# Sparse attention layer of a decoder trunk: compressed tokens and gate columns as weights with hi and lo halves side by side, compressed keys appended to the first keys

## The chip, the cores and the metric

The kernel runs on one core of a Trainium2 chip. The metric is the device time of one execution in microseconds (us); the time of a kernel is the median of its runs. The engines are named TensorE (PE; its weight loads PEld), VectorE (DVE), ScalarE (ACT), GpSimd (POOL) and SyncE (SP, which issues the weight transfers).

## What is computed

Four decoder layers over 256 tokens of width 2048: stick-breaking attention, native sparse attention, gated spatial mixing, stick-breaking attention again. Each layer adds its mixer's output and a gated projection of a per-layer input to `x`. The change is in the second layer, the sparse attention (16 heads in 4 groups of 4 that share keys and values), of which this matters:

```python
# compressed keys and values: 15 blocks of 32 tokens, stride 16
def compress_blocks(kv, blk_idx, pos, w1, w2):
    blocks = kv[:, blk_idx] + pos[:, None, :]
    flat = blocks.transpose(0, 1, 3, 2, 4).reshape(B, n_cmp, G, CMP_LEN * Dh)
    return gelu(flat @ w1) @ w2
gates = sigmoid(g).reshape(B, S, 3, G, HG)
s_c = einsum('bqgnd,bcgd->bgnqc', qf, kc) - slopes * dist_c      # 15 compressed keys
p_c = softmax(where(mask_c, s_c, NEG)) * mask_c
s_s = einsum('bqgnd,bgqtd->bgnqt', qf, k_g) - slopes * dist_s    # selected keys
s_w = einsum('bqgnd,bkgd->bgnqk', qf, k_b) - slopes * dist_w     # window keys
o = gate_c * (p_c @ vc) + gate_s * (p_s @ v_s) + gate_w * (p_w @ v_w)
y = (o * silu(z)) @ w_out
```

All is float32 in the reference. The kernel keeps that precision on TensorE by splitting an operand into a rounded part (hi, type fp32r) and the rest (lo), and adding the products hi*hi, hi*lo and lo*hi.

## The kernel before, in words

**Units.** The whole program is a list of units. A unit is 1024 columns of a weight array: SyncE loads two units with one transfer (`load`), `cut` splits a unit into `wh` (ScalarE copy, L80) and `wl` (VectorE subtraction, L81), and a function issues its matmuls. `run` walks the units in order. At unit `i` it first issues the cuts up to unit `i + 3` (`SPLIT_AHEAD = 3`, four buffers, so that cut `i + 3` waits until TensorE is done with unit `i - 1`), then calls `resume`, then issues the unit's own matmuls. `resume` takes one step in each open generator, the oldest first. A `yield` in a generator so ends its part of one unit. All engines execute in the order in which this walk issues. One such stop, from one unit to the next, is called a step below.

**Tiles.** `fm` computes 128 output features for 256 tokens with two units, each of 8 pairs of matmuls of 512 and 256 columns (L212, L214), and hands the sum in PSUM to a generator: `joined` adds its two halves (ScalarE L248, VectorE L249), `scaled` multiplies by the norm (L255). `tm` computes values, token-major, with 8 units of 12 matmuls (L236 to L238).

**The sparse layer** (`nsa`). First come 8 units of values, the four tiles of keys to be compressed (`cmp_tiles(0)`), 8 units of values, the four compression units of the keys (`cmp_units(0)`), the four tiles and later the four units of the values to be compressed, and between them the gate columns (`gate_unit`, 16 pairs on 48 output rows). `cmp_post` adds the positions to the last tile's windows (VectorE, 8 instructions, L692) and `cmp_unit` multiplies with float32 weights that are not cut: 8 matmuls of 60 columns for each unit, which appear as 16 instructions (L707).

**The heads.** Then 16 heads follow. Each has the two units of its query tile and two units of a fill tile (a gate tile `z` for heads 3, 4, 6, 7, 8, 10 to 15, else a key tile). Its generator `q_post` and `attend` take one step for each of these parts:

- 0: query scaled; 1: query split; 2: nothing
- 3: scores on TensorE into PSUM banks A and B: three 512-column and three 256-column matmuls, and two float32 ones of 15 columns against `kc` (L837)
- 4: VectorE adds slopes and takes the maxima (L853, L855); 5: six exponentials on ScalarE (L863)
- 6: VectorE scales the probabilities (L866 to L875); 7: nothing
- 8: TensorE transposes them into banks C and D (L887, L888); 9: nothing
- 10: banks C and D are copied out in turns, ScalarE `ptc`, VectorE `ptc`, ScalarE `pt`, VectorE `pt`, ScalarE `pt1`, first C, then D (L89, L91, L80, L81, L897); 11: nothing
- 12: product with the values (TensorE, bank E, L903 to L907); 13: output copied (L911)

A head takes four steps, so that its neighbour is always four steps behind it: with steps named after the head's own number modulo four, step 0 holds one head's query, the next older head's maxima and the transposes of the one before, and so on. `z_post` multiplies the output by the gate on GpSimd once it is there, and splits it.

Of the kernel before, what the change touches and what calls it, by code (L numbers as in the profile page):

```python
# [16 lines left out]
P = 128  # L17
# [8 lines left out]
NCMP = 15  # L26
CMP_LEN = 32
# [13 lines left out]
class Trunk:  # L41
# [576 lines left out]
    def nsa(self, layer, act_in, act_out):  # L618
# [10 lines left out]
        def begin():  # L629
# [4 lines left out]
            st["kc"] = m.tile([P, G, NCMP], F32, name="kc")  # L634
# [24 lines left out]
            st["raw"] = [c.tile([P, G, S], F32, name=f"raw{b}") for b in range(2)]  # L659
            st["pos"] = [c.tile([P, CMP_LEN], F32, name=f"pos{b}") for b in range(2)]  # L660
            st["w2"] = [c.tile([P, HD], F32, name=f"w2{b}") for b in range(2)]
            st["h3"] = c.tile([P, G, 4, 32], F32, name="h3")
# [15 lines left out]
        def cmp_post(b, g):  # L678
            def gen(ps):
                t = st["raw"][b]  # L680
                self.scaled(ps, self.rb, t[:, g])
                if g == G - 1:

                    x = st["c"].tile([P, CMP_LEN, G, NCMP], F32, name="win")
                    st["win", b] = x
                    half = CMP_STRIDE
                    for i in range(CMP_LEN // half):
                        src = t[:, :, i * half:i * half + NCMP * half].rearrange(
                            "p g (c l) -> p l g c", l=half)
                        ps_ = st["pos"][b][:, i * half:(i + 1) * half]  # L690
                        for g2 in range(G):
                            nc.vector.tensor_add(  # L692
                                x[:, i * half:(i + 1) * half, g2], src[:, :, g2],
                                ps_[:, :, None].to_broadcast([P, half, NCMP]))
                return
                yield
            return gen

        def cmp_unit(b, q):
            def pe(raw, _):  # L700
                if q == 0:
                    st["cps", b] = self.bank("AB"[b])
                ps = st["cps", b]
                n = G * NCMP
                for j in range(8):
                    l = 8 * q + j
                    mm(ps[:, :n], raw[:, j * P:(j + 1) * P],  # L707
                       st["win", b][:, l].rearrange("p g c -> p (g c)"), start=l == 0,
                       stop=l == CMP_LEN - 1)
                if q == 3:  # L710
                    self.bg.append(cmp_gen(b, ps))
            return pe

        def cmp_gen(b, ps):
            n = G * NCMP
            if b == 0:
                h = st["c"].tile([P, n], F32, name="cmp_h")
                nc.scalar.activation(h, ps[:, :n], AF.Gelu)
            else:
                h3 = st["h3"]  # L720
                h = ps[:, :n].rearrange("p (g c) -> p g c", g=G)
# [36 lines left out]
        def gate_unit(wh, wl):  # L758
            n = 3 * H
            ps = self.acc.tile([P, 2, S], F32, name="acc")  # L760
            for k in range(KT):
                c = slice(k * n, (k + 1) * n)
                mm(ps[:n], wh[:, c], act_in[:, k], start=k == 0, stop=False,
                   skip_group_check=True)
                mm(ps[:n, 0], wl[:, c], act_in[:, k, 0], start=False, stop=k == KT - 1,
                   skip_group_check=True)
            self.bg.append(gate_post(ps))

        def gate_post(ps):
            n = 3 * H  # L770
            t = st["c"].tile([n, S], F32, name="g_lo")
            e = st["c"].tile([n, S], F32, name="g")
            nc.scalar.activation(t, ps[:n, 1], AF.Copy)
            nc.vector.tensor_add(e, ps[:n, 0], t)
            nc.vector.tensor_mul(e, e, self.rb[:n])
            nc.scalar.activation(e, e, AF.Exp, scale=-1.0)
            nc.vector.tensor_scalar(e, e, 1.0, None, op0=ALU.add)
# [47 lines left out]
        def attend(h, q, qs):  # L825
# [5 lines left out]
            kh, kl = keys(g)  # L831
            self.mm3(sa.rearrange("p (b s) -> p b s", b=2), (qs[:, 0, P:], qs[:, 1, P:]), (kh, kl),
                     start=True, stop=True)
            self.mm3(sb[:, :S].rearrange("p (b s) -> p b s", b=2), (qs[:, 0, :P], qs[:, 1, :P]),
                     (kh[:, :, :P], kl[:, :, :P]), start=True)
            for i in range(2):
                mm(sb[:, S + i * NCMP:S + (i + 1) * NCMP], q[:, i * P:(i + 1) * P], st["kc"][:, g],  # L837
                   start=False, stop=i == 1, skip_group_check=True)
# [11 lines left out]
                     sb[:, S:S + 2 * NCMP].rearrange("p (b s) -> p b s", b=2), mx[:, :, 0]))  # L850
# [81 lines left out]
        self.unit(a["nsa_g"], KT * 3 * H, gate_unit)  # L932
# [205 lines left out]
```

## Time and profile before

| | us |
|---|---|
| median of 3 runs | 2246.32 (2246.31 to 2246.91) |
| the profiled execution's own time | 2246.55 |
| its span in the profile | 2244.8 |
| TensorE busy | 2220.6 (99%) |
| VectorE busy | 1490.7 (66%) |
| ScalarE busy | 1227.8 (55%) |
| TensorE's granted clock over the span | 0.998 of full speed |

The profile is of one execution. Busy time is the time in which an engine has an instruction in work; matmuls are pipelined, so that the distance from one start to the next, not the duration, tells what one costs. A wait is idle time and what ended it. The chain of waits follows the work that ended last back to its start.

### The profile page before, as it was taken

Reading aid. Unit: us, or ns where it says so; the run is one execution under the profiler, and the core shown is the slowest. Engines: PE = TensorE matmul, PEld = TensorE weight load, DVE = VectorE, ACT = ScalarE, POOL = GpSimd, SP = SyncE. Lnnn points to the kernel's source line nnn. Section 1 sums busy time; section 2 is a strip of 40 time slices with the busy share of each in tenths; the row PEclk is TensorE's granted clock in tenths of the full one; section 3 lists DMA queues with packets and bytes.
Section 4 is the critical chain, followed back from the end, with each engine's and each line's share of the span. In section 5 each row is a group of like instructions: output and inputs, shape, how many; then the busy total and the mean of one; then the engine's idle time right before and its main releaser. Section 6 shows DMA issues by size and latency. Waiting matters only on the chain.

```text
span 2244.8 us, 32505 instructions
## 1 busy us (share of the span) xinstructions
PE 2220.6 (99%) x12664; PEld 1940.8 (86%) x12664; DVE 1490.7 (66%) x2242; ACT 1227.8 (55%) x2031; POOL 187.1 (8%) x203
## 2 busy tenths in 40 slices
PE   8999999999999999999999999999999999999997
PEld 6888888888888888888888888888888888888886
DVE  7655656657656788886675566666766566567666
ACT  6555556546544566654555555544555555555464
POOL 2000000002200011230121000000310000000022
PEclk9999999999999999999999999999999999999999
DMA  7455454555555434345556555555554544445552
GB/s 255 164 187 169 170 175 163 188 188 187 195 188 197 149 140 151 132 169 188 187 186 222 193 174 188 172 188 186 189 191 169 188 165 173 171 167 188 188 188 104
DMA packets 106522, 400.13 MB, mean 178 GB/s; under 512 B 7936, under 2 KB 8448, under 8 KB 106112
## 3 DMA queue, kind: packets, MB, share of 16 engines
q1 hardware_dynamic: 105792, 397.34, 51.2%
q8 instruction: 100, 1.64, 0.3%
q10 hardware_dynamic: 576, 0.70, 0.1%
q14 instruction: 54, 0.44, 0.1%
HBM read 395.92 MB, written 2.10 MB: 177 GB/s over the span
## 4 chain that ended last, share of the span: by engine, by line
PE 91%; DVE 4%; ACT 3%; issue 1%; DMA 0%; DVEq 0%; SPq 0%; ACTq 0%
PE acc L212 47%; PE acc L214 24%; PE acc L236 4%; PE acc L237 4%; PE acc L238 4%; DVE wl L81 1%; ACT wh L80 1%; ACT p L863 1%; PE ps_A L96 1%; PE ps_A L97 1%; PE ps_A L98 0%; PE ps_B L96 0%; PE ps_B L98 0%; PE ps_B L97 0%; DVE p L875 0%
## 5 line engine op out<-in xcount | busy, mean ns | idle before, releaser
L212 PE MATMUL acc<-act,wh 128*128 128x512 f32 x4864 | 1719.4, 395 | 0.0
L214 PE MATMUL acc<-act,wl 128*128 128x256 f32 x4864 | 1374.6, 283 | 0.0
L81 DVE TENSOR_TENSOR wl<-raw,wh 128x1024 fp32r<-128x1024 f32 (+1 forms) x738 | 927.7, 1261 | 596.8 <-ACT wh L80 596.5
L80 ACT ACTIVATE wh<-raw 128x1024 fp32r<-128x1024 f32 (+1 forms) x738 | 776.5, 1056 | 790.1 <-PE acc L212 459.2
L212 PEld LDWEIGHTS acc<-act,wh 128*128 128x128 f32 x4864 | 913.7, 188 | 206.2
L214 PEld LDWEIGHTS acc<-act,wl 128*128 128x128 f32 x4864 | 914.7, 188 | 0.4
L236 PE MATMUL acc<-wh,act 128*128 128x512 f32 x448 | 178.5, 398 | 5.9 <-ACT wh L80 5.9
L237 PE MATMUL acc<-wl,act 128*128 128x512 f32 x448 | 178.1, 397 | 2.1 <-DVE wl L81 2.1
L238 PE MATMUL acc<-wh,act 128*128 128x512 f32 x448 | 177.2, 396 | 0.0
L321 POOL TENSOR_TENSOR ssq<-x 128x256 f32<-128x256 f32 x4 | 2.5, 616 | 1459.7 <-DVE x L449 1459.7
L236 PEld LDWEIGHTS acc<-wh,act 128*128 128x128 f32 x448 | 84.8, 189 | 25.1 <-ACT wh L80 5.9
L237 PEld LDWEIGHTS acc<-wl,act 128*128 128x128 f32 x448 | 84.7, 189 | 23.6 <-DVE wl L81 5.0
L238 PEld LDWEIGHTS acc<-wh,act 128*128 128x128 f32 x448 | 84.7, 189 | 19.6
L248 ACT ACTIVATE t_lo<-acc 128x256 f32<-128x256 f32 x240 | 88.2, 368 | 8.6 <-PE acc L214 8.6
L249 DVE TENSOR_TENSOR t_join<-acc,t_lo 128x256 f32<-128x256 f32 x176 | 73.0, 415 | 1.7 <-ACT t_lo L248 1.6
L325 POOL TENSOR_TENSOR ssq<-ssq,sq 128x256 f32<-128x256 f32 x59 | 60.6, 1028 | 4.6
L324 POOL TENSOR_TENSOR sq<-x 128x256 f32<-128x256 f32 x59 | 40.1, 679 | 227.2 <-DVE x L449 227.2
L814 POOL TENSOR_TENSOR th<-th,z 128x256 f32<-128x256 f32 x16 | 18.7, 1167 | 339.6 <-ACT th L812 339.6
L84 DVE SCALAR_TENSOR_TENSOR act<-x,gv,act 128x256 fp32r<-128x256 f32 x64 | 41.5, 658 | 6.9 <-ACT act L83 6.9
L539 ACT ACTIVATE e<-e 128x384 f32<-128x384 f32 x32 | 16.8, 525 | 40.1 <-DVE e L538 40.1
L83 ACT ACTIVATE act<-x,gv 128x256 fp32r<-128x256 f32 x64 | 31.1, 497 | 13.8 <-DVE x L449 10.6
L81 DVE TENSOR_TENSOR act<-o,act 128x512 fp32r<-128x512 f32 (+1 forms) x32 | 20.0, 626 | 19.8 <-ACT act L80 19.8
(292 smaller groups left out, 1643.6 us busy)
## 6 DMA issues: line engine op xcount, KB each, us to landing
raw<-in_sb_qkz SPq DMA_DIRECT2D x80, 1024.0 KB, 4.9
raw<-in_ple_gate SPq DMA_DIRECT2D x53, 1024.0 KB, 4.8
raw<-in_sb_w_out SPq DMA_DIRECT2D x30, 1024.0 KB, 4.8
raw<-in_nsa_fm SPq DMA_DIRECT2D x29, 1024.0 KB, 4.9
raw<-in_gm_uz SPq DMA_DIRECT2D x28, 1024.0 KB, 4.8
raw<-in_sb_v SPq DMA_DIRECT2D x24, 1024.0 KB, 4.8
raw<-in_nsa_fm SPq DMA_DIRECT2D x38, 512.0 KB, 4.0
raw<-in_sb_qkz SPq DMA_DIRECT2D x32, 512.0 KB, 4.0
```

Source lines behind the costliest of these rows:

```text
L80: nc.scalar.activation(hi, src, AF.Copy)
L81: nc.vector.tensor_sub(lo, src, hi.bitcast(F32))
L84: nc.vector.scalar_tensor_tensor(lo, src, scale, hi.bitcast(F32), op0=ALU.mult, op1=ALU.subtract)
L212: mm(ps, wh[:, j * P:(j + 1) * P], act[:, k], start=k == 0, stop=False, skip_group_check=True)
L214: mm(ps[:, 0], wl[:, j * P:(j + 1) * P], act[:, k, 0], start=False, stop=k == KT - 1, skip_group_check=True)
L236: mm(ps, act[:, k, 0, t], w_h, start=k == 0, stop=False)
L237: mm(ps, act[:, k, 0, t], w_l, start=False, stop=False)
L238: mm(ps, act[:, k, 1, t], w_h, start=False, stop=k == KT - 1)
L248: self.nc.scalar.activation(t, ps[:, 1], AF.Copy)
L249: self.nc.vector.tensor_add(out, ps[:, 0], t)
L324: nc.gpsimd.tensor_mul(sq, self.x[:, k], self.x[:, k])
L325: nc.gpsimd.tensor_add(self.ssq, self.ssq, sq)
```

## The change

Four edits, all in the sparse layer:

1. **Compression.** `cmp_post` makes the windows as a hi and a lo part side by side, 32 times one ScalarE and one VectorE instruction of 60 elements, in four steps of 8. The cmp units are now cut like the others, into one tile `w` with both halves. `cmp_unit` takes the windows (120 columns) as weights and both halves of `w` (256 columns) as the moving operand: 8 matmuls for each unit. `cmp_gen` adds the halves (ScalarE, VectorE) and folds hi and lo by a matmul with `sum2`.
2. **Gate.** The gate columns are cut so that hi and lo of each of the 16 parts lie side by side (96 columns); 16 matmuls of 512 columns replace 16 pairs. `gate_post` folds hi and lo with `sumg` where it transposed, and applies norm and exponential afterwards.
3. **Scores.** For each group of heads, `attend` copies the first 128 columns of both key blocks and the split `kc` into a tile `kb` (three ScalarE instructions, one VectorE), and the 256-column matmuls become 272 columns wide, which hold the first half's compressed scores. One float32 matmul against `kc` is left.
4. **A step more.** After it fills `kb`, the generator of a group's first head yields, so that its scores come at its step 4 and all that follows is one step later than in the other three heads.

```diff
         if split:
-            wh = self.wp.tile([P, 1024], F32R, name="wh", bufs=SPLIT_AHEAD + 1)
-            wl = self.wp.tile([P, 1024], F32R, name="wl", bufs=SPLIT_AHEAD + 1)
-            for t in self.pieces(self.n_cut, cols):
-                self.split(wh[:, t], wl[:, t], raw[:, t])
-            self.ops[self.n_cut] = (wh, wl)
+            w = self.wp.tile([P, 2, 1024], F32R, name="w", bufs=SPLIT_AHEAD + 1)
+            wh, wl = w[:, 0], w[:, 1]
+            if split == "rows":
...
+                self.split(wv[:, :, 0], wv[:, :, 1],
+                           raw[:, :cols].rearrange("p (k n) -> p k n", n=n))
+            else:
+                for t in self.pieces(self.n_cut, cols):
+                    self.split(wh[:, t], wl[:, t], raw[:, t])
+            self.ops[self.n_cut] = (wh, wl) if split is True else (w,)
...
-                    for i in range(CMP_LEN // half):
...
-                        for g2 in range(G):
-                            nc.vector.tensor_add(
...
+                    for l in range(CMP_LEN):
...
+                        nc.scalar.activation(win[:, l, 0], src, AF.Identity, bias=pos)
+                        nc.vector.scalar_tensor_tensor(win[:, l, 1], src, pos,
+                                                       win[:, l, 0].bitcast(F32), op0=ALU.add,
+                                                       op1=ALU.subtract)
+                        if l % 8 == 7:
+                            yield
...
-                    mm(ps[:, :n], raw[:, j * P:(j + 1) * P],
-                       st["win", b][:, l].rearrange("p g c -> p (g c)"), start=l == 0,
-                       stop=l == CMP_LEN - 1)
+                    mm(ps[:2 * NW, :2 * P].rearrange("p (a b) -> p a b", a=2),
+                       st["win", b][:, l].rearrange("p a g c -> p (a g c)"),
+                       w[:, :, j * P:(j + 1) * P], start=l == 0, stop=l == CMP_LEN - 1)
...
+            nc.scalar.activation(t, ps[:n, P:2 * P], AF.Copy)
+            nc.vector.tensor_add(y, ps[:n, :P], t)
+            yield
+            o = self.bank("C")
+            mm(o[:, :NW], y, st["sum2"][:n], start=True, stop=True)
...
-                mm(ps[:n], wh[:, c], act_in[:, k], start=k == 0, stop=False,
-                   skip_group_check=True)
-                mm(ps[:n, 0], wl[:, c], act_in[:, k, 0], start=False, stop=k == KT - 1,
-                   skip_group_check=True)
+                mm(ps[:2 * n], w[:, 2 * k * n:2 * (k + 1) * n], act_in[:, k], start=k == 0,
+                   stop=k == KT - 1, skip_group_check=True)
...
+            if h % (H // G) == 0:
+                kb = st["kb"] = m.tile([P, 2, S + 16], F32R, name="kb")
+                for i, k in enumerate((kh, kl)):
+                    nc.scalar.activation(kb[:, i, :S].rearrange("p (b s) -> p b s", b=2),
+                                         k[:, :, :P].bitcast(F32), AF.Copy)
+                self.split(kb[:, 0, S:], kb[:, 1, S:], st["kc"][:, g])
+                yield
+            kb = st["kb"]
...
-            self.mm3(sb[:, :S].rearrange("p (b s) -> p b s", b=2), (qs[:, 0, :P], qs[:, 1, :P]),
-                     (kh[:, :, :P], kl[:, :, :P]), start=True)
-            for i in range(2):
-                mm(sb[:, S + i * NCMP:S + (i + 1) * NCMP], q[:, i * P:(i + 1) * P], st["kc"][:, g],
-                   start=False, stop=i == 1, skip_group_check=True)
+            self.mm3(sb[:, :S + 16], (qs[:, 0, :P], qs[:, 1, :P]), (kb[:, 0], kb[:, 1]),
+                     start=True, stop=True)
+            mm(sb[:, S + 16:S + 32], q[:, P:], st["kc"][:, g], start=False, stop=True,
+               skip_group_check=True)
...
-                self.unit(a["cmp_w1"][b, q], 1024, cmp_unit(b, q), split=False)
+                self.unit(a["cmp_w1"][b, q], 1024, cmp_unit(b, q), split="both")
...
-        self.unit(a["nsa_g"], KT * 3 * H, gate_unit)
+        self.unit(a["nsa_g"], KT * 3 * H, gate_unit, split="rows")
```

How this moves instructions, at three places. **ScalarE at head 8, the first of the third group.** Before, its exponentials (`p_8064`, `pc`) are followed by the copies of head 7's transposes out of banks C and D:

```order
L863 ACTIVATE p_8064,sm<-p_8064,mx 128x256
L863 ACTIVATE p_8065,sm<-p_8065,mx 128x128
L863 ACTIVATE pc,sm<-pc,mx 128x15
L80 ACTIVATE act_73<-o 128x256
L80 ACTIVATE qs<-q 128x256
L80 ACTIVATE wh<-raw 128x1024
L89 ACTIVATE ptc<-ps_C 128x128
L80 ACTIVATE pt<-ps_C 128x256
L897 ACTIVATE pt_8103<-ps_C 128x128
L89 ACTIVATE ptc<-ps_D 128x128
L80 ACTIVATE pt<-ps_D 128x256
L897 ACTIVATE pt_8103<-ps_D 128x128
```

Now they come after these copies, in the same step (`p_7978` is the same head's):

```order
L90 ACTIVATE ptc<-ps_C 128x128
L81 ACTIVATE pt<-ps_C 128x256
L933 ACTIVATE pt_7959<-ps_C 128x128
L90 ACTIVATE ptc<-ps_D 128x128
L81 ACTIVATE pt<-ps_D 128x256
L933 ACTIVATE pt_7959<-ps_D 128x128
L899 ACTIVATE p_7978,sm<-p_7978,mx 128x256
L899 ACTIVATE p_7979,sm<-p_7979,mx 128x128
L899 ACTIVATE pc,sm<-pc,mx 128x15
L899 ACTIVATE p_7978,sm<-p_7978,mx 128x256
L899 ACTIVATE p_7979,sm<-p_7979,mx 128x128
L899 ACTIVATE pc,sm<-pc,mx 128x15
```

The first head's exponentials moved behind the older head's copies and one cut (`w`, before `wh`) further back. **TensorE at the transposes of head 9**, the head behind it, before, with the engines that a row waits for in brackets:

```order
L887 MATMUL ps_C<-ident,p_8242 128x128 [waits DVE_49,PE_49]
L887 MATMUL ps_C<-ident,p_8241 128x128 x2
L888 MATMUL ps_C<-ident,pc_5522 128x128 [waits DVE_49]
L887 MATMUL ps_D<-ident,p_8242 128x128 [waits DVE_49,PE_49]
L887 MATMUL ps_D<-ident,p_8241 128x128 x2
L888 MATMUL ps_D<-ident,pc_5522 128x128 [waits DVE_49]
```

and now:

```order
L923 MATMUL ps_C<-ident,p_8106 128x128 [waits PE_49,Activation_49]
L923 MATMUL ps_C<-ident,p_8105 128x128 x2
L924 MATMUL ps_C<-ident,pc_5324 128x128
L923 MATMUL ps_D<-ident,p_8106 128x128 [waits PE_49,Activation_49]
L923 MATMUL ps_D<-ident,p_8105 128x128 x2
L924 MATMUL ps_D<-ident,pc_5324 128x128
```

The wait for VectorE's scaled probabilities became a wait for ScalarE, which reads banks C and D last: head 8's copies are issued one step ahead of these transposes, where two lay between. **ScalarE from the last part of the value windows to the unit after the second compression**, before (`g` is the gate, the three cuts belong to units after the compression):

```order
L773 ACTIVATE g_lo<-acc 48x256
L776 ACTIVATE g<-g 48x256
L248 ACTIVATE t_lo<-acc 128x256
L80 ACTIVATE wh<-raw 128x1024
L80 ACTIVATE act_73<-t_join 128x256
L80 ACTIVATE wh<-raw 128x1024 x3
```

and now:

```order
L709 ACTIVATE win<-raw,pos_5344 128x60 x8
L81 ACTIVATE w<-raw 128x1024
L709 ACTIVATE win<-raw,pos_5344 128x60 x8
L808 ACTIVATE gate<-ps_D,nrt 128x48 x2
L257 ACTIVATE t_lo<-acc 128x256
L81 ACTIVATE w<-raw 128x1024
L81 ACTIVATE act_73<-t_join 128x256
L81 ACTIVATE w<-raw 128x1024 x3
```

The cut of the last compression unit, a window part and the gate's exponentials now stand ahead of the cut of the unit behind the compression.

## Rows read from the trace of the kernel before

**Rows 1.** Page, parts 1 and 4: engines' busy time; chain by engine.

```profile
PE 2220.6 (99%) x12664; PEld 1940.8 (86%) x12664; DVE 1490.7 (66%) x2242; ACT 1227.8 (55%) x2031; POOL 187.1 (8%) x203
...
PE 91%; DVE 4%; ACT 3%; issue 1%; DMA 0%; DVEq 0%; SPq 0%; ACTq 0%
```

**Rows 2.** Waits: engine, tile, line, releaser: us total, times, longest.

```profile
PE ps_E L903 <- DVE ptc L91: 1.4, 1, 1.4
```

**Rows 3.** Chain that ended last, in the heads: start us, us, what.

```profile
841.65 1.05 ACT wh L80
...
856.76 1.05 ACT wh L80
```

**Rows 4.** TensorE's timeline: start us, us, engine, line, operation, out<-in, form, count.

```profile
659.33 7.25 PE L707 MATMUL ps_A<-win,raw 128*128 128x60 f32 x64
...
835.83 0.52 PE L837 MATMUL ps_B<-kc,q 128*128 128x15 f32 x4
...
849.65 0.40 PE L96 MATMUL ps_A<-act,qs 128*128 128x512 f32 x1
...
850.35 0.28 PE L96 MATMUL ps_B<-act,qs 128*128 128x256 f32 x1
...
850.71 0.52 PE L837 MATMUL ps_B<-kc,q 128*128 128x15 f32 x4
851.07 0.48 PE L212 MATMUL acc<-act,wh 128*128 128x512 f32 x1
...
853.95 0.28 PE L903 MATMUL ps_E<-ptc,vc 128*128 128x256 f32 x1
...
855.22 0.49 PE L887 MATMUL ps_C<-ident,p 128*128 128x128 f32 x3
...
856.01 0.48 PE L212 MATMUL acc<-act,wh 128*128 128x512 f32 x1
...
925.48 0.51 PE L837 MATMUL ps_B<-kc,q 128*128 128x15 f32 x4
...
940.58 0.51 PE L837 MATMUL ps_B<-kc,q 128*128 128x15 f32 x4
```

**Rows 5.** VectorE's timeline in one head's turn; in brackets the idle time before.

```profile
844.04 0.67 DVE L853 SCALAR_TENSOR_TENSOR p<-d,ps_A 128x512 f32<-128x512 f32 x1
...
846.08 0.41 DVE L249 TENSOR_TENSOR t_join<-acc,t_lo 128x256 f32<-128x256 f32 x1
...
846.86 1.22 DVE L81 TENSOR_TENSOR wl<-raw,wh 128x1024 fp32r<-128x1024 f32 x1
...
849.88 1.23 DVE L81 TENSOR_TENSOR wl<-raw,wh 128x1024 fp32r<-128x1024 f32 x1 [0.50 <-ACT wh L80]
851.13 0.28 DVE L91 TENSOR_TENSOR ptc<-ps_C,ptc 32x128 fp32r<-32x128 f32 x1
...
853.88 0.18 DVE L866 RECIPROCAL sm<-sm 128x6 f32<-128x6 f32 x1
...
855.53 0.41 DVE L249 TENSOR_TENSOR t_join<-acc,t_lo 128x256 f32<-128x256 f32 x1
```

**Rows 6.** ScalarE's timeline in the same turn.

```profile
845.83 0.51 ACT L863 ACTIVATE p<-p,mx 128x256 f32<-128x256 f32 x1 [0.33 <-DVE mx L855]
...
848.19 0.40 ACT L80 ACTIVATE act<-o 128x256 fp32r<-128x256 f32 x1
...
854.00 0.28 ACT L897 ACTIVATE pt<-ps_D 128x128 f32<-128x128 f32 x1 [0.49 <-DVE pt L81]
```

**Rows 7.** ScalarE's and VectorE's timelines ahead of the heads.

```profile
660.25 2.00 ACT L80 ACTIVATE wh<-raw 128x1024 fp32r<-128x1024 f32 x2
...
661.34 2.36 DVE L81 TENSOR_TENSOR wl<-raw,wh 128x1024 fp32r<-128x1024 f32 x2 [1.17 <-ACT wh L80]
...
700.76 0.76 DVE L785 RECIPROCAL gate<-ps_D 128x96 f32<-128x96 f32 x1 [3.82 <-PE ps_D L782]
...
712.72 0.45 ACT L723 ACTIVATE h<-ps_B 128x60 f32<-128x60 f32 x3
```

More of the change, by code (lines that the diff above doesn't have):

```diff
@@ L26 @@
 NCMP = 15
+NW = G * NCMP
 CMP_LEN = 32
@@ L633, in begin @@
             st["v1"] = m.tile([P, 2, 512], F32, name="v1")
-            st["kc"] = m.tile([P, G, NCMP], F32, name="kc")
+            st["kc"] = m.tile([P, G, 16], F32, name="kc")
+            nc.gpsimd.memset(st["kc"], 0.0)
             st["vc"] = m.tile([P, G * HD], F32R, name="vc")
@@ L658, in begin @@
             c = st["c"] = self.open_pool("cmp")
-            st["raw"] = [c.tile([P, G, S], F32, name=f"raw{b}") for b in range(2)]
             st["pos"] = [c.tile([P, CMP_LEN], F32, name=f"pos{b}") for b in range(2)]
             st["w2"] = [c.tile([P, HD], F32, name=f"w2{b}") for b in range(2)]
+            for name, n in (("sum2", NW), ("sumg", 3 * H)):
+                st[name] = c.tile([P, n], F32, name=name)
+                nc.gpsimd.tensor_add(st[name], self.ident[:, :n], self.ident[:, n:2 * n])
+            st["nrt"] = c.tile([P, 2], F32, name="nrt")
             st["h3"] = c.tile([P, G, 4, 32], F32, name="h3")
@@ L679, in gen @@
             def gen(ps):
-                t = st["raw"][b]
+                if g == 0:
+                    st["raw", b] = st["c"].tile([P, G, S], F32, name="raw")
+                t = st["raw", b]
                 self.scaled(ps, self.rb, t[:, g])
                 if g == G - 1:
-                    x = st["c"].tile([P, CMP_LEN, G, NCMP], F32, name="win")
-                    st["win", b] = x
+                    win = st["c"].tile([P, CMP_LEN, 2, G, NCMP], F32R, name="win")
+                    st["win", b] = win
                     half = CMP_STRIDE
-                    for i in range(CMP_LEN // half):
-                        src = t[:, :, i * half:i * half + NCMP * half].rearrange(
-                            "p g (c l) -> p l g c", l=half)
-                        ps_ = st["pos"][b][:, i * half:(i + 1) * half]
-                        for g2 in range(G):
-                            nc.vector.tensor_add(
-                                x[:, i * half:(i + 1) * half, g2], src[:, :, g2],
-                                ps_[:, :, None].to_broadcast([P, half, NCMP]))
+                    for l in range(CMP_LEN):
+                        o = l // half * half
+                        src = t[:, :, o:o + NCMP * half].rearrange(
+                            "p g (c l) -> p l g c", l=half)[:, l - o]
+                        pos = st["pos"][b][:, l:l + 1]
+                        nc.scalar.activation(win[:, l, 0], src, AF.Identity, bias=pos)
[4 more added lines that the diff above has]
+                            yield
                 return
@@ L714, in cmp_gen @@
         def cmp_gen(b, ps):
-            n = G * NCMP
+            n = 2 * NW
+            t = st["c"].tile([n, P], F32, name="cmp_lo")
+            y = st["c"].tile([n, P], F32, name="cmp_sum")
+            nc.scalar.activation(t, ps[:n, P:2 * P], AF.Copy)
[3 more added lines that the diff above has]
+            mm(o[:, :NW], y, st["sum2"][:n], start=True, stop=True)
             if b == 0:
-                h = st["c"].tile([P, n], F32, name="cmp_h")
-                nc.scalar.activation(h, ps[:, :n], AF.Gelu)
+                h = st["c"].tile([P, NW], F32, name="cmp_h")
+                nc.scalar.activation(h, o[:, :NW], AF.Gelu)
             else:
                 h3 = st["h3"]
-                h = ps[:, :n].rearrange("p (g c) -> p g c", g=G)
+                h = o[:, :NW].rearrange("p (g c) -> p g c", g=G)
                 for i in range(3):
@@ L726, in cmp_gen @@
             yield
-            yield
+            n = NW
             o = self.bank("C")
@@ L770, in gate_post @@
             n = 3 * H
[L771 to L777, printed above, removed]
+            t = st["c"].tile([2 * n, S], F32, name="g_lo")
+            e = st["c"].tile([2 * n, S], F32, name="g")
+            nc.scalar.activation(t, ps[:2 * n, 1], AF.Copy)
+            nc.vector.tensor_add(e, ps[:2 * n, 0], t)
+            nc.vector.tensor_scalar(st["nrt"], self.r[:, S:], -1.0, None, op0=ALU.mult)
             yield
@@ L781, in gate_post @@
             for i in range(2):
-                nc.tensor.transpose(ps[:, i * n:(i + 1) * n], e[:, i * P:(i + 1) * P],
-                                    self.ident[:n, :n])
+                mm(ps[:, i * n:(i + 1) * n], e[:, i * P:(i + 1) * P], st["sumg"][:2 * n],
+                   start=i == 0, stop=i == 1, skip_group_check=True)
+            for i in range(2):
+                nc.scalar.activation(st["gate"][:, i].rearrange("p b h -> p (b h)"),
+                                     ps[:, i * n:(i + 1) * n], AF.Exp,
+                                     scale=st["nrt"][:, i:i + 1])
             g = st["gate"].rearrange("p i b h -> p (i b h)")
-            nc.vector.reciprocal(g, ps[:, :2 * n])
+            nc.vector.tensor_scalar(g, g, 1.0, None, op0=ALU.add)
+            nc.vector.reciprocal(g, g)
             nc.vector.tensor_scalar(st["gate"][:, 0, 0], st["gate"][:, 0, 0], st["valid"], None,
```

15 lines of the change are left out of this document (9 added, 6 removed).

## Prediction

> **What bounds the kernel now.** I read the page first: TensorE is busy 99% of the span and 91% of the chain of waits lies on it [rows 1]. So a microsecond taken from TensorE counts, unless something else is about to end last. The waits say where that is: over the whole span TensorE waits for VectorE inside the sparse heads, 1.4 us at the product with the values in the last turn [rows 2]. The chain, read in order of time, leaves TensorE in this stretch: it repeats the same ScalarE and VectorE pieces every 856.76 − 841.65 = 15.11 us [rows 3]. TensorE's scores come every 850.71 − 835.83 = 14.88 us in the middle of the heads and every 940.58 − 925.48 = 15.10 us near their end [rows 4]. The reader is to see that two engines that are each busy some two thirds of the time need more per head, in their fixed order, than the full TensorE does: each waits for the other in turn. They fall behind by 0.23 us a head until TensorE stands still for them. What decides this change is its effect on that order, more than TensorE's own columns.
>
> **TensorE's work.** Distances from start to start, [rows 4] throughout:
> - Compression: 64 half matmuls took 7.25 us, twice 14.5 us. Now 64 matmuls of 256 columns. Three such take 850.71 − 850.35 = 0.36 us, 0.12 each: 7.7 us. Gain 6.8 us. The weights are 120 columns wide instead of 128. I see no reason for less than 0.12 (as many moving columns), and the upper bound is the 512-column price, (850.35 − 849.65) / 3 = 0.23, which would add 7 us; the moving length is that of the cheaper row.
> - Gate: a pair costs (853.95 − 851.07) / 8 = 0.36 us, a 512-column matmul alone 0.23; with the pair at its 0.35 without the first one's delay, 16 × 0.12 = 1.9 us gained.
> - The new folds: two float32 matmuls of 60 columns for the compressions (0.11 for a half, 0.23 each) and two for the gate in place of two transposes, together 0.7 us lost.
> - Heads: four halves against `kc` took 851.07 − 850.71 = 0.36 us; two remain, and 48 columns more cost 0.02. Gain 0.16 × 16 = 2.6 us.
>
> Together 10.6 us, of which 8.0 ahead of the heads.
>
> **Ahead of the heads.** Where the compression units were not cut, ScalarE and VectorE had a pause. Now each unit needs 1.06 and 1.2 us there, and TensorE consumes one in 8 × 0.12 = 0.96 us. *First compression*: ScalarE is done with the value tile at 660.25, so that is where the fourth unit's cut starts; VectorE's share ends at 661.34 + 1.18 = 662.5 [rows 7]. TensorE starts at 659.33 and needs 2.9 us for three units: a wait of 0.3, and 0.2 for the unit behind. Its fold needs VectorE after five cuts and a sum, 661.34 + 5.9 + 0.3 = 667.5; TensorE is there at 666.5: 1.0. *Second compression*, clock at TensorE's arrival: cut 1.1 + 1.2, last window part 1.2, the gate's addition, reciprocal (0.76 before) and mask 1.1, a join and its product 0.8, cut 1.2: the unit behind is ready at 6.6, TensorE at 0.4 + 32 × 0.12 = 4.2, wait 2.4. Its fold: VectorE at 6.6 + 0.4 + 3 × 1.2 + 0.3 = 10.9, TensorE at 6.6 + 2.85 = 9.45, wait 1.5. Sum of waits 5.4, so the stretch gains 2.6 us.
>
> For a window instruction I took 0.15 us, from three ScalarE ones of 60 columns in 0.45 [rows 7]; the other bound is the 0.28 of a 128-column copy [rows 6], 1 us more for the part that counts. [...]
>
> **A group's first head.** Its scores, and all behind them, come one step later. I walk the order through with VectorE's start-to-start times [rows 5]: cut 1.2, maxima 846.08 − 844.04 = 2.04, join and product 846.86 − 846.08 = 0.78, copies of banks C and D from 851.13 to ScalarE's end at 854.28, 3.15, reciprocal and scaling 855.53 − 853.88 = 1.65; six exponentials 848.19 − 845.83 = 2.36 [rows 6]. TensorE [rows 4]: product with the values 855.22 − 853.95 = 1.27, transposes 0.79, scores 1.42 before and 1.26 now, hence a unit (14.88 − 1.42 − 1.27 − 0.79) / 4 = 2.85. The clock starts where TensorE releases the buffer for the cut in the step of the first head's maxima.
>
> - *First wait: its own scaling.* ScalarE and VectorE: cut 1.1 + 1.2, maxima 2.04, two splits 0.7, cut 1.2, the older head's copies 3.15; only then, in the same step, the exponentials 2.36, with VectorE idle behind the next join, 0.4; join 0.8, cut 1.2, reciprocal and first half 1.05. First half ready at 15.2, the second at 15.85. TensorE until the transposes: four units 11.4, scores 1.25, product 1.27: 13.9. Wait 1.3 and 0.2.
> - *Second wait: banks C and D.* From 15.85 VectorE has 0.35, cut 1.2, maxima 2.04, join 0.8, cut 1.2, then 1.0 for the query split behind ScalarE's exponentials, 0.6 behind its cut, cut 1.2, scaling 1.65, join 0.8, cut 1.2, and only then this head's copies: C is free at 29.3, D at 31.0. TensorE: transposes until 16.2, two units 21.9, held 0.5 by the query split, scores and a unit until 26.5. The next head's transposes want C there: 2.8, then D 1.3. Before, a whole step more lay between.
> - *Third wait*: the product of the head after that. VectorE: 2.5 for cut and cut, a turn of 15.1, 10.2 from maxima to the end of the copies (844.04 to 854.28), 1.1 behind a cut that TensorE releases late: 59.9. TensorE: 0.4, eight units 22.8, two products 2.54, scores 1.25, transposes 0.79: 58.8. Wait 1.1.
> - *Fourth*: the next group's `kb` copies (two of 0.3 us, a split) stand behind a cut in ScalarE's order while TensorE is already at the scores: 0.6. As VectorE's and ScalarE's work they lie in ScalarE's pause ahead of `z`.
>
> Sum 7.8 us per group. Off go TensorE's 4 × 0.16 and the 4 × 0.23 it already lost: 6.3 net for the second and third group. In the first group the engines start without arrears and the first wait falls away (banks 2.6, third and fourth 1.7, less 0.6): 3.7. The last has no next group, and the 1.6 us at the end that it already lost are in it: 7.2 − 0.6 − 0.9 − 1.6 = 4.1. Heads: 3.7 + 6.3 + 6.3 + 4.1 = 20.4 us longer.
>
> **Sum.** The profiled execution took 2246.55 us, 0.23 above the median of 2246.32: the two are the same for this purpose. 2246.55 − 2.6 + 20.4 = **2264 us**. From no change I'd tell 0.2%, 4.5 us.
>
> **The rivals.**
> - *TensorE stays the end*: the walk is too pessimistic, the arrears that were harmless until the twelfth head swallow the late step too. Then nearly all of the 10.6 us counts, less 5.4 ahead of the heads at the most: 2236 to 2242 us. For it speaks the 99% [rows 1]; against it that TensorE's pace in the last heads is already that of the others [rows 3, 4], so that the heads' 2.6 us can't show. Its point is whether the copies of C and D end within one unit and the scores, 2.85 + 1.25 us, after TensorE's release; a cut on both engines and the copies alone are 1.1 + 1.2 + 3.15 = 5.45. [...] Chance 0.10.
> - *Only the copies count*: the two engines catch up in between, and each group pays 5.45 − 4.1 = 1.35 at the banks, the 1.5 at its own scaling, 0.6 at `kb`, about 3.4: 2246.55 − 2.6 + 3.4 × 4 − 1.5 = 2256 us. Chance 0.18.
> - *More arrears than walked*: each wait also delays the release of weight buffers, so that the next turn starts later on ScalarE; with half as much again in the heads, 2246.55 − 2.6 + 30.6 = 2275 us. Chance 0.10.
> - *The compression doesn't get cheaper* (0.23 for a matmul): 2271 us with the rest as forecast; it is inside the range and takes no chance of its own.
>
> **How the numbers follow.** The forecast has 0.62, with 2258 to 2272 as its own range. The range of 2250 to 2276 takes in the second rival and most of the third and leaves out the first. Faster by over 0.2% is the first rival, 0.09; within 0.2% are its rest and the low end of the second, 0.04; slower 0.87.
>
> **What would show it.** In the changed profile: the compression's 32 matmuls at 0.12 us; TensorE's waits at the transposes into ps_C and ps_D, for ScalarE's copies (`pt`) at heads 1, 5, 9, 13, some 4 us at the last three, and for VectorE's scaling at 4, 8, 12; some 66 us from head 4's scores to head 8's where four turns take 60 now; a wait of over 2 us behind the second compression. The forecast is wrong if the heads take as long as before, or if TensorE's waits there sum to less than 10 us.

## The result: 2278.19 us, 1.4% slower

The changed kernel takes 2278.19 us (median of four runs, 2277.52 to 2279.34) against 2246.32 (2246.13 to 2246.91): ratio 1.0141, 95% interval 1.0128 to 1.0153. That is 31.9 us more where 17.7 were forecast; the direction was right, the size was not: 2278 lies above the forecast's range. The profiled execution spans 2276.3 us (2244.8 before), so the trace holds 31.5 of it.

The page of the changed kernel, part 1 and the chain by engine, answering to [rows 1]:

```profile
PE 2224.6 (98%) x12558; PEld 1937.2 (85%) x12558; DVE 1512.6 (66%) x2304; ACT 1255.4 (55%) x2118; POOL 184.6 (8%) x206
...
PE 91%; DVE 5%; ACT 3%; issue 1%; DMA 0%; DVEq 0%; SPq 0%; ACTq 0%
```

By the records TensorE has 106 matmuls fewer and is busy longer. The page alone would let one look for dearer matmuls; the waits and the clock tell more.

**The forecast waits are there.** TensorE's waits in the whole span (total, times, longest), where before there were in this layer the one of [rows 2] and one of 0.2 us for the scaled probabilities:

```profile
PE ps_C L923 <- ACT pt L933: 8.1, 4, 2.9
PE ps_C L923 <- DVE p L911: 6.3, 7, 2.8
...
PE ps_D L923 <- ACT pt L933: 4.1, 4, 1.0
PE ps_B L98 <- DVE kb L82: 3.5, 3, 1.2
...
PE acc L223 <- DVE w L82: 1.9, 1, 1.9
PE ps_E L939 <- DVE ptc L92: 1.6, 4, 0.8
...
PE ps_B L726 <- DVE win L710: 1.3, 1, 1.3
PE ps_C L742 <- DVE cmp_sum L739: 0.8, 1, 0.8
PE ps_D L805 <- DVE nrt L800: 0.8, 1, 0.8
```

**What was not forecast: the clock.** Busy time by stretch: the stretch and its length, then busy us and count of PE, PEld, DVE, ACT and POOL, the granted clock, the DMA share and GB/s:

```profile
700.00:705.90 5.90, 3.86 (x21) 2.82 (x20) 5.47 (x19) 5.05 (x14) 0.00 (x0) 1.00 0.50 178
705.90:712.40 6.50, 4.93 (x16) 4.26 (x17) 5.51 (x7) 3.42 (x5) 0.00 (x0) 0.50 0.58 214
818.90:820.60 1.70, 0.32 (x2) 0.00 (x0) 1.63 (x6) 1.70 (x3) 0.00 (x0) 1.00 0.00 0
820.60:831.50 10.90, 10.89 (x64) 9.26 (x64) 9.70 (x27) 5.74 (x19) 0.00 (x0) 1.00 0.55 194
831.50:835.60 4.10, 0.83 (x6) 0.42 (x4) 2.66 (x6) 1.21 (x4) 0.00 (x0) 1.00 0.35 82
835.60:839.00 3.40, 2.73 (x10) 2.45 (x11) 1.81 (x2) 1.80 (x4) 2.25 (x3) 0.50 0.52 212
...
903.90:910.70 6.80, 5.79 (x20) 5.05 (x20) 4.90 (x10) 2.04 (x5) 3.06 (x3) 0.50 0.32 131
...
961.90:965.30 3.40, 3.40 (x13) 2.92 (x12) 3.37 (x9) 0.99 (x5) 0.00 (x0) 0.50 0.21 87
```

In four stretches TensorE is granted 0.50, where before it had 1.00 in this whole stage (640 to 1010 us). Each follows a place where it stood still: the second compression, and the transposes of heads 5, 9 and 12. Behind the 1.4 us pause of head 4 (818.90 to 820.60) it kept 1.00. What half clock does to a unit's matmuls, from TensorE's timeline (start, busy):

```profile
837.82 0.63 PE L221 MATMUL acc<-act,w 128*128 128x512 f32 x1
...
838.46 0.63 PE L221 MATMUL acc<-act,w 128*128 128x512 f32 x1
...
839.43 0.40 PE L221 MATMUL acc<-act,w 128*128 128x512 f32 x1
...
839.79 0.39 PE L221 MATMUL acc<-act,w 128*128 128x512 f32 x1
```

A pair starts 0.64 us behind the last one at half clock and 0.36 at full. The longest stretch in the heads shows what that adds up to. The transposes into ps_D and the eight pairs behind them take 824.52 − 821.22 = 3.30 us behind head 4's pause and 910.89 − 904.97 = 5.92 behind head 9's:

```profile
821.22 0.55 PE L923 MATMUL ps_D<-ident,p 128*128 128x128 f32 x3
...
824.52 0.40 PE L221 MATMUL acc<-act,w 128*128 128x512 f32 x1
...
904.97 0.90 PE L923 MATMUL ps_D<-ident,p 128*128 128x128 f32 x3 [1.01 <-ACT pt L933]
...
910.89 0.28 PE L939 MATMUL ps_E<-ptc,vc 128*128 128x256 f32 x1
```

Counted so, against the same instructions at 1.00, the four stretches cost TensorE 2.2, 1.3, 2.6 and 1.5 us: 2.2 ahead of the heads and 5.4 in them.

At 0.50, half of TensorE's busy time in the four stretches, 16.8 us, would be an estimate of 8.4 us for this loss; the rows give 7.6, and run e9 below shows that less than that is to be had back.

**Where the 31.5 us lie.** Two events mark the ends of the stage: the second compression's last product, at 716.33 before and 718.37 after, and the last transposes, at 975.84 and 1006.75. So 2.0 us come ahead of the heads and 28.9 in them. The last matmul of the scores of heads 4, 8 and 12 after, then of heads 4 and 12 before (head 8: 850.71, [rows 4]):

```profile
802.24 0.29 PE L872 MATMUL ps_B<-kc,q 128*128 128x16 f32 x2
...
870.94 0.29 PE L872 MATMUL ps_B<-kc,q 128*128 128x16 f32 x2
...
941.01 0.29 PE L872 MATMUL ps_B<-kc,q 128*128 128x16 f32 x2
```

```profile
791.20 0.51 PE L837 MATMUL ps_B<-kc,q 128*128 128x15 f32 x4
...
910.38 0.51 PE L837 MATMUL ps_B<-kc,q 128*128 128x15 f32 x4
```

The second group takes 68.70 us (59.51 before), the third 70.07 (59.67). The first runs from the product to head 4's scores, the last from head 12's scores to the last transposes; head 4's and 12's scores now have a unit, a product and transposes more ahead of them (2.80 + 1.27 + 0.79 = 4.86 us), which is taken from the one and added to the other: 83.87 − 74.87 − 4.86 = 4.1 and 65.74 − 65.46 + 4.86 = 5.1.

| Stage | Forecast, us | Measured, us | Lost by TensorE at half clock |
|---|---|---|---|
| ahead of the heads | −2.6 | +2.0 | 2.2 |
| heads, first group | 3.7 | 4.1 | 0 |
| second group | 6.3 | 9.2 | 1.3 |
| third group | 6.3 | 10.4 | 2.6 |
| last group | 4.1 | 5.1 | 1.5 |

### The profile page after: what moved, and what is told of

It is laid out like the page before. It is cut to its first block, busy times and chain, and to the rows that moved or that the text cites. A ratio compares the mean times of both kernels' runs of the same rounds, so it can differ in the third digit from the quotient of the medians.

```text
span 2276.3 us, 32101 instructions
## 1 busy us (share of the span) xinstructions
PE 2224.6 (98%) x12558; PEld 1937.2 (85%) x12558; DVE 1512.6 (66%) x2304; ACT 1255.4 (55%) x2118; POOL 184.6 (8%) x206
## 4 chain that ended last, share of the span: by engine, by line
PE 91%; DVE 5%; ACT 3%; issue 1%; DMA 0%; DVEq 0%; SPq 0%; ACTq 0%
PE acc L221 47%; PE acc L223 24%; PE acc L245 4%; PE acc L246 4%; PE acc L247 4%; DVE w L82 2%; ACT w L81 1%; PE ps_B L98 1%; PE ps_A L97 0%; PE ps_B L97 0%; PE ps_A L98 0%; PE ps_A L99 0%; ACT p L899 0%; PE ps_B L99 0%; DVE pt L82 0%
## 5 line engine op out<-in xcount | busy, mean ns | idle before, releaser
L221 PE MATMUL acc<-act,w 128*128 128x512 f32 x4864 | 1726.5, 396 | 0.4 <-ACT w L81 0.4
L223 PE MATMUL acc<-act,w 128*128 128x256 f32 x4864 | 1377.7, 283 | 1.9 <-DVE w L82 1.9
L82 DVE TENSOR_TENSOR w<-raw,w 128x1024 fp32r<-128x1024 f32 (+1 forms) x746 | 938.5, 1263 | 605.7 <-ACT w L81 604.7
L81 ACT ACTIVATE w<-raw 128x1024 fp32r<-128x1024 f32 (+1 forms) x746 | 784.6, 1056 | 805.4 <-PE acc L223 487.5
L221 PEld LDWEIGHTS acc<-act,w 128*128 128x128 f32 x4864 | 917.3, 189 | 207.5 <-ACT w L81 0.6
L223 PEld LDWEIGHTS acc<-act,w 128*128 128x128 f32 x4864 | 918.2, 189 | 2.7 <-DVE w L82 2.2
L245 PE MATMUL acc<-w,act 128*128 128x512 f32 x448 | 178.6, 399 | 6.1 <-ACT w L81 6.1
L246 PE MATMUL acc<-w,act 128*128 128x512 f32 x448 | 178.1, 398 | 1.5 <-DVE w L82 1.5
L247 PE MATMUL acc<-w,act 128*128 128x512 f32 x448 | 177.2, 396 | 0.0
L245 PEld LDWEIGHTS acc<-w,act 128*128 128x128 f32 x448 | 84.8, 189 | 25.5 <-ACT w L81 6.1
L246 PEld LDWEIGHTS acc<-w,act 128*128 128x128 f32 x448 | 84.8, 189 | 22.9 <-DVE w L82 4.3
L247 PEld LDWEIGHTS acc<-w,act 128*128 128x128 f32 x448 | 84.7, 189 | 19.7
L548 ACT ACTIVATE e<-e 128x384 f32<-128x384 f32 x32 | 16.8, 525 | 40.1 <-DVE e L547 40.1
L84 ACT ACTIVATE act<-x,gv 128x256 fp32r<-128x256 f32 x64 | 31.1, 497 | 13.7 <-DVE x L458 10.7
```

Of the source, the lines that this page charges most:

```text
L81: nc.scalar.activation(hi, src, AF.Copy)
L82: nc.vector.tensor_sub(lo, src, hi.bitcast(F32))
L221: mm(ps, wh[:, j * P:(j + 1) * P], act[:, k], start=k == 0, stop=False, skip_group_check=True)
L223: mm(ps[:, 0], wl[:, j * P:(j + 1) * P], act[:, k, 0], start=False, stop=k == KT - 1, skip_group_check=True)
L245: mm(ps, act[:, k, 0, t], w_h, start=k == 0, stop=False)
L246: mm(ps, act[:, k, 0, t], w_l, start=False, stop=False)
```

## The experiments

The theory going in: the heads lose by the late step and the clock behind its waits; ahead of the heads the small window instructions make ScalarE and VectorE late. Each kernel ran beside the kernel before (medians 2246.56 to 2246.64).

**e1: the empty step alone.** Into the kernel before:

```
+            if h % (H // G) == 0:
+                yield
```

> The kernel before, with nothing added but one empty step ahead of the scores of heads 0, 4, 8 and 12 (no copy, no other matmul). Theory A (the late step alone makes the waits): of the 28.9 us that the changed heads lost, the 3 x 1.16 us at kb fall away and the 2.6 us that the shorter scores gave are not there, so about +26 to +28 us, 2272 to 2275, with the waits of 2.9 us at ps_C for pt at heads 5 and 9 and a granted clock of 0.50 behind them. Rival B (the copies into kb and their wait make the loss, and the step costs nothing): within 4.5 us of 2246.

Measured: 2272.87 us, ratio 1.0118 (1.0103 to 1.0133), +26.3. TensorE's waits in the heads:

```profile
PE ps_C L889 <- ACT pt L899: 8.7, 4, 2.7
PE ps_C L889 <- DVE p L877: 5.3, 7, 2.4
PE ps_D L889 <- ACT pt L899: 3.1, 4, 1.0
```

These are the changed kernel's waits, with nothing of its new work there, and the granted clock is 0.50 behind those of heads 5 and 9 here too (832 to 838 and 900 to 906 us). B falls: the step costs it, not what is done in it.

**e2: the heads' part of the change alone** (`kb`, shorter scores, empty step).

> The kernel before with the change's kb, shorter scores and empty step, and with the old compression and gate. Theory A (the loss lies in the heads): about +29 us, 2275. Rival C (half of the loss comes from ahead of the heads, by engines that arrive late at the first head): +15 us, 2261.

Measured: 2273.39 us, 1.0121 (1.0104 to 1.0137), +26.8. The loss lies in the heads; C falls. The loss is no smaller than e1's, but TensorE also waits 3.5 us for `kb` here, so this run does not tell what the shorter scores bring; e7 does.

**e3: the compression and gate alone** (scores as before).

> The change's compression and gate with the scores of before. Theory A: the two traces put the same work 2.0 us later at the second compression's last product, and the heads hide none of it and add nothing: +1 to +3 us, 2247 to 2249. Rival D (the forecast's own sum for this part): -2.6 us, 2244. Rival E (the 8.0 us of TensorE's work all count): 2238.

Measured: 2248.55 us, 1.0009 (1.0000 to 1.0019), +1.9. Theory A; D and E fall.

**e4: `kb` filled one step ahead.** In `q_post`, with the empty step gone from `attend`:

```
                 self.split(qs[:, 0], qs[:, 1], q)
                 yield
+                if h % (H // G) == 0:
+                    ...
+                    self.split(kb[:, 0, S:], kb[:, 1, S:], st["kc"][:, g])
                 yield
                 yield from attend(h, q, qs)
```

> The change, with kb filled one step ahead of the scores, in a step where the head has nothing to do, and without the empty step. Theory A: the 28.9 us of the heads go; what stays is the 2 us ahead of the heads, less what the shorter scores give, plus what ScalarE and VectorE lose to three fills of 0.8 us: 2244 to 2252, no clock of 0.50 in the heads. Rival B (the fill itself costs): 2265 or more, with waits for kb or pt at each group's first heads.

Measured: 2268.15 us, 1.0096 (1.0081 to 1.0111). A's number was wrong by 16 us; the time lies in B's range. ScalarE's timeline around the fill for head 4, and TensorE's scores:

```profile
793.01 0.25 ACT L90 ACTIVATE ptc<-ps_C 128x128 fp32r<-128x128 f32 x1
...
797.26 0.28 ACT L933 ACTIVATE pt<-ps_D 128x128 f32<-128x128 f32 x1 [0.49 <-DVE pt L82]
797.43 0.71 ACT L833 ACTIVATE kb<-act 128x256 fp32r<-128x256 f32 x2
798.05 0.20 ACT L81 ACTIVATE kb<-kc 128x16 fp32r<-128x16 f32 x1
```

```profile
798.30 0.39 PE L97 MATMUL ps_B<-kb,qs 128*128 128x272 f32 x1 [4.34 <-ACT kb L81]
```

In that step the older head's copies out of ps_C and ps_D stand ahead of the fill and take ScalarE from 793.01 to 797.4. TensorE waits 4.3 us for a fill that itself takes under 1 us, and is granted 0.50 from 799.5 to 802.5. So theory A can be right only with the place: early in steps is not early in ScalarE's order.

**e6: `kb` two steps ahead**, right behind the split of the query, before those copies.

> The change without the empty step, with kb filled two steps ahead of the scores, behind the split of the head's query and ahead of the copies out of ps_C and ps_D that delayed it in the run with one step. Theory A (only lateness for TensorE costs): no wait for kb, no clock of 0.50 in the heads, 2246 to 2252. Rival B (the 0.9 us of ScalarE and 0.2 of VectorE per group cost several times their length in every place): 2262 or more.

Measured: 2249.81 us, 1.0015 (1.0005 to 1.0025). The fill is the same as in e4, the place differs: 2268 us one step ahead of the scores, 2250 two. (The change's 2278 has the late step besides.) The clock stays at 1.00 in the heads: no 512-column matmul takes over 0.48 us there, where those at 0.50 in the changed kernel took 0.63. B falls.

**e7: as e6, the two long copies on GpSimd** (`nc.gpsimd.tensor_copy`).

> As the run before it, with the two long copies into kb on GpSimd, which is busy 8%. Theory A: as that run or up to 3 us less, since ScalarE keeps 0.6 us per group. Rival I (GpSimd's copies are slow, or it comes to them late behind a head's z): a wait for kb ahead of the scores of heads 4, 8 and 12, and more than that run.

Measured: 2248.27 us, 1.0006 (0.9997 to 1.0016). No wait for `kb`; 1.5 us less than e6. Beside e3's 2248.55 this says that the shorter scores bring nothing, even where `kb` costs nothing: from head 0's scores to head 15's both kernels take 220.42 us. In e7 the scores come every 14.7 us at first, but from head 5 on every 15.0 on the mean, close to the 15.1 us turn of the two other engines.

**e5: TensorE's idle time filled.** Matmuls that nobody reads, ahead of the transposes.

> The change, with matmuls of 256 columns (0.12 us each) that add nothing put where TensorE stands still ahead of the transposes of heads 4, 5, 8, 9, 12 and 13: 10, 22, 10, 22, 22 and 10 ahead of those into ps_C, and 8 ahead of ps_D at 5, 9 and 13. Nobody reads what they write. Theory F (behind its pauses TensorE is granted half its clock, and what it then computes at 0.43 in place of 0.23 us counts): the granted clock stays at 1.00 from 720 to 1010 us, and of the 12 us that it was busy at half clock there 6 come back: 2271 to 2274. Rival G (the slow stretches only take up waits that come anyway): within 2 us of the change's 2278. Rival H (the added matmuls delay what stands behind them): 2281 or more.

Measured: 2289.03 us, 1.0188 (1.0173 to 1.0203); H, and no answer on the clock. I had put the matmuls of heads 4, 8 and 12 into ps_A, which was still being read by the next head's maxima:

```profile
PE ps_A L925 <- DVE p L889: 13.7, 3, 5.3
```

**e9: the same in banks that are free there.**

```
             for b in range(2):
                 ps = self.bank("CD"[b])
+                d = self.bank("E") if h in (5, 9, 13) and b == 0 else d if b else ps
+                for i in range(n_fill.get(h, (0, 0))[b]):
+                    mm(d[:, :S], ..., act_in[:, i % KT, 0], start=True, stop=True)
```

> As the run that filled TensorE's idle time, with the added matmuls in banks that are free at that place: at heads 4, 8 and 12 (where TensorE waits for the scaled p, not for a bank) in ps_C itself, ahead of the transposes that overwrite it; at heads 5, 9 and 13 (where it waits for the bank ps_C) in ps_E, which the next product with the values overwrites. 10, 22, 10, 22, 22, 10 and three times 8 as before. Theory F (half clock behind the pauses costs 6 us in the heads): granted clock 1.00 from 720 to 1010 us and 2271 to 2275. Rival G (the slow stretches only take up waits that come anyway): within 2 us of the change's 2278. A fill that leaves the clock low says nothing for either.

Measured: 2274.58 us, 1.0123 (1.0108 to 1.0138), runs from 2273.77 to 2275.24: below all runs of the changed kernel, by 3.6 us between medians. The two ratios' intervals overlap a little, so I lean on the trace, where the clock is 1.00 through the heads:

```profile
831.50:835.60 4.10, 3.81 (x31) 3.56 (x30) 2.91 (x7) 0.96 (x4) 0.00 (x0) 1.00 0.21 45
835.60:839.00 3.40, 3.34 (x24) 2.92 (x23) 1.52 (x2) 2.05 (x5) 1.84 (x3) 1.00 0.64 261
...
903.90:910.70 6.80, 6.74 (x45) 5.99 (x44) 5.32 (x10) 4.65 (x14) 3.08 (x3) 1.00 0.21 84
```

Head 4's to head 8's scores take 67.44 us (68.70 in the changed kernel), 8 to 12 take 67.45 (70.07); the last stretch is the same (65.79 and 65.74). So TensorE's idling does bring the low clock here (1.00 with these pauses filled, 0.50 without), and F holds at the edge of its range. Of the 5.4 us some 3.9 come back: 1.3 and 2.6 in the second and third group, all that the rows give there. In the last group nothing does: head 12's two units take 5.69 us for 7.22, and head 13's transposes start their next unit as late as before, behind ScalarE's copies.

**e8: windows in 8 + 8 + 8 instructions of 240 columns** (sum and lo part on VectorE, hi on ScalarE, one buffer for the sum), `kb` as in e6.

```
-                    for l in range(CMP_LEN):
+                    for l in range(0, CMP_LEN, 4):
...
+                        nc.vector.tensor_add(x, src, pos)
+                        self.split(win[:, c, 0], win[:, c, 1], x)
```

> kb filled two steps ahead, and the windows made by 8 + 8 + 8 instructions of 240 columns in place of 32 + 32 of 60. Theory J (ahead of the heads the 7.7 us of waits come from some 8 us of small window instructions on each of two engines): the waits for win and for the cut behind the second compression shrink to under 3 us together and the clock stays at 1.00 there, so 4 to 6 us less than with kb alone: 2240 to 2247. Rival K (the cuts of the eight compression units make those waits): no more than 1 us less.

Measured: 2258.08 us, 1.0052 (1.0037 to 1.0067): 8.3 more than e6. Groups by line and form (count, busy us, mean ns):

```profile
L712 DVE TENSOR_TENSOR x<-raw,pos 128x240 f32<-128x240 f32 x16 | 9.1, 571 | 0.3
...
L82 DVE TENSOR_TENSOR win<-x,win 128x240 fp32r<-128x240 f32 x16 | 6.5, 408 | 7.5 <-ACT win L81 7.5
L81 ACT ACTIVATE win<-x 128x240 fp32r<-128x240 f32 x16 | 6.5, 404 | 24.2 <-DVE x L712 24.2
```

With one buffer the three follow one another, 0.57 + 0.40 + 0.41 us for four windows where 4 × 0.29 (ScalarE's pace, below) had been enough. Both numbers were wrong, J's and K's. That slower windows cost 8 us shows that the time to make them decides this stretch; that it is the smallness of the instructions, as J says, it doesn't show.

**e10: the second compression later.** As e7, with `k_tile(1, 0)` ahead of `cmp_units(1)`, and the change of pools between the two units of head 0's query.

> kb on GpSimd two steps ahead (the run of 2248.3 us) and the second compression behind the tile of keys that used to follow it, so that TensorE has 5.6 us more between the last window's input and its use. Theory J (ScalarE and VectorE are late at the second compression by the small window instructions): the waits for win (2.9 us) and for the cut behind it (2.1) go or fall under 1.5 together, the clock stays at 1.00 there: 2241 to 2245. Rival M (they are late by their whole load ahead of the heads, and the wait only moves): 2247 or more.

Measured: 2245.57 us, 0.9996 (0.9987 to 1.0006), between J's range and M's. The clock is 1.00 there and the wait for win is gone, but J's gain is not all there: other waits for VectorE take its place. (The traced execution took 2246.85 us, 1.3 above the median.)

```profile
PE ps_C L742 <- DVE cmp_sum L739: 2.0, 2, 1.2
PE ps_B L726 <- DVE w L82: 1.7, 2, 1.4
```

**e11: and the windows' sums on GpSimd**, into two buffers.

> As the run before it, with the windows' sums on GpSimd (8 + 8 instructions of 240 columns into two buffers), so that ScalarE and VectorE have 8 each of 240 columns instead of 32 of 60 per compression. Theory J: also the 0.9 us for nrt and 0.5 for the first cut go: 2238 to 2243, the fastest of all. Rival I (GpSimd needs over 1 us for one): waits for win, 2246 or more.

Measured: 2243.84 us, 0.9987 (0.9978 to 0.9996): 2.8 us below the kernel before, the only version whose interval lies below 1, and 0.8 us above J's range. The wait for nrt is gone, the 0.5 for the first cut is not.

**e12: GpSimd's sums with the compression at the change's place.**

> As that, with the second compression at the change's place. Theory J: 2242 to 2246. Rival I: 2250 or more, with TensorE waiting for win as in the run with the windows in 8 + 8 + 8 instructions on VectorE and ScalarE.

Measured: 2247.47 us, 1.0004 (0.9994 to 1.0014), between J and I: the waits for win and the cut are 1.4 and 1.2 us, and the clock still falls behind them, to 0.50 from 703.5 to 709.5 us. The place counts for 3.6 us (beside e11), the instructions alone for 0.8 (beside e7). So larger window instructions by themselves give back little, though VectorE's part of them took 393 to 917 ns, with a median of 477, where the mean in e8 was 408 (last section). Whether the small instructions (J) or the load of ScalarE and VectorE as a whole (M) make the waits ahead of the heads is not settled.

## Why the forecast was too small

*Held.* The bound: two engines in a fixed order decide, TensorE's columns don't (e7). The compression's 256 columns at 0.12 us: 24 in the 3.08 us of the row below, 6.5 us gained of 6.8. The gate's 1.8 of 1.9. The late step as the cause: e1 shows it by itself. The heads' waits, which I check by starts in the second group: first wait 1.55 us (forecast 1.3 + 0.2), banks C and D 3.08 + 1.04 (2.8 + 1.3), third group of waits 0.9 (1.1), `kb` 1.3 (0.6), the query's split not seen (0.5): 7.9 for 7.8. The third group's waits are the same to 0.02 us. "Only the copies count", "TensorE stays the end" and the dearer compression are out. "More arrears than walked" has nearly the right time for another reason: the arrears are as walked.

*The step that failed: what a wait costs.* "Sum 7.8 us per group. Off go TensorE's 4 × 0.16 and the 4 × 0.23 it already lost: 6.3 net" takes a wait at its own length and TensorE's work behind it at its old price. Rows of the changed kernel show that price at 0.64 for a pair instead of 0.36 behind the longer waits. In the heads that is 5.4 us by rows, of which 3.9 count by e9. The second part of that sentence was wrong too: before, TensorE had not lost 0.23 a head in the middle groups; its 14.88 us [rows 4] were its own work, and it stood still only in the last turn [rows 2]. That took 0.92 too much off each of the two. The last group's sum, 7.2 − 0.6 − 0.9 − 1.6, seems to take it off once more, beside the 1.6 us of waits that rows do show; without it the sum is 5.0, and 5.1 was measured. So 2.8 us of wrong subtraction and 3.9 of clock are 6.7 of the 8.5 us that the heads missed by.

*Ahead of the heads* the sum of waits was mis-sized, and the clock left out. TensorE's timeline at the second compression:

```profile
697.88 0.62 PE L805 MATMUL ps_D<-sumg,g 96*128 96x48 f32 x4 [0.77 <-DVE nrt L800]
698.32 3.08 PE L726 MATMUL ps_B<-w,win 128*120 128x256 f32 x24
702.71 1.96 PE L726 MATMUL ps_B<-w,win 128*120 128x256 f32 x8 [1.32 <-DVE win L710]
705.10 0.50 PE L221 MATMUL acc<-act,w 128*128 128x512 f32 x1 [0.42 <-ACT w L81]
707.47 0.58 PE L223 MATMUL acc<-act,w 128*128 128x256 f32 x1 [1.88 <-DVE w L82]
```

and ScalarE's and VectorE's beside it:

```profile
697.92 1.23 DVE L82 TENSOR_TENSOR w<-raw,w 128x1024 fp32r<-128x1024 f32 x1
699.06 1.90 DVE L710 SCALAR_TENSOR_TENSOR win<-raw,pos,win 128x60 fp32r<-128x60 f32 x8
...
701.09 2.10 ACT L709 ACTIVATE win<-raw,pos 128x60 fp32r<-128x60 f32 x7
...
702.36 1.89 DVE L710 SCALAR_TENSOR_TENSOR win<-raw,pos,win 128x60 fp32r<-128x60 f32 x8
```

The last eight matmuls take 1.96 us where eight of the 24 ahead of them took 1.0: they follow VectorE's last eight window instructions one by one. When TensorE began with the gate's fold, at 697.88, VectorE still had a cut, a window part, the next cut and the last part ahead of it, until 704.25; the walk counted one cut on each engine and one part of 1.2 us, 3.5 together. From start to start the compression takes 6.78 us for 3.84 of work, 2.9 of waiting that I had not seen at all (0.4 of it for the next unit's cut); the unit behind it waits 2.1 (2.4 forecast), the gate's fold 0.9 (none), the first compression 0.7 and its fold 1.0 (0.5 and 1.0), the second fold nothing (1.5, but TensorE came later). Sum 7.7 for 5.4. Beside the part left out, the term mis-sized is the window instruction: I took 0.15 us from three that read PSUM. VectorE needs 0.23 from start to start ((1.89 − 0.31) / 7 with 0.31 for one), ScalarE 0.29 (seven in 2.10 us, 0.38 for one).

All of it: 4.6 us ahead of the heads (2.2 of clock, 2.3 of waits) and 6.7 in them, of the 13.7 us by which the traces miss the forecast. Open are 1.8 us in the heads, 0.4 to 0.7 in each group but the last, and 0.6 behind them.

How long the low clock stays isn't fixed by the pauses: heads 5 and 9 show the same waits of 2.92 and 1.01 us, and 3.4 and 6.8 us of 0.50 behind them. In e2 the stretch in the third group is shorter, some 3.4 us between 902.2 and 905.9, and the group with it, 68.76 us for 70.07. That is most of what the changed heads lose beyond e2's. What sets the length stays open.

## What to carry to other kernels

Where a full engine is bound by the order of two others, ask of a change first which generator it moves by a step (an empty step alone cost 26 us, e1), and what stands ahead of the moved instruction in each engine's order: with the same 0.9 us fill the kernel stood 22 us above the one before where it was issued one step ahead of its use, and 3 us where it was two. Price a stall of TensorE as its length plus what follows at half clock (here, in the heads, 3.4 to 6.8 us at 0.50 behind pauses of 2.8 us and more), as far as no other engine is late there anyway, and read the granted clock behind every pause, not only the page's mean. An engine's arrears count as lost only where the busiest engine is seen to wait for them.

## What the runs showed of the hardware that I had not expected

- The clock falls in the middle of a busy kernel: in the heads of the changed kernel it is 0.50 for 3.4 to 6.8 us behind a pause of 2.77 us (head 12) and behind pauses of 2.92 and 1.01 us together (heads 5 and 9), and 1.00 behind those of 1.39 us (heads 4 and 8). Matmuls that nobody reads, put into the pauses, kept it at 1.00 in the heads (e9).
- GpSimd beside VectorE: in e11, with the sums on GpSimd, VectorE's equal 240-column subtractions took from 394 to 926 ns (duration min/median/max):

```profile
L711 POOL TENSOR_TENSOR x<-raw,pos x16: 707/724/1807, 640.3 to 700.1; 128x240 f32<-128x240 f32 x16
...
L82 DVE TENSOR_TENSOR win<-x,win x16: 394/670/926, 641.5 to 702.4; 128x240 fp32r<-128x240 f32 x16
```

In e8, with GpSimd without work there, the mean was 408. One that ran beside a sum of GpSimd's, at 650.34, takes 0.93 us, with GpSimd at work from 649.20 to 651.01; the next, at 651.48 with GpSimd idle, 0.41. So part of what GpSimd took over came back as longer instructions.
